# Ten early pairs per layer, later sums for the modulations, and a norm in seventeen steps

## The chip, the cores and the metric

The kernel runs on one core of a Trainium2 chip. The metric is the device time of one launch in microseconds (us). Five engines run their own streams of instructions: TensorE (PE in the profile; its weight loads are PEld), VectorE (DVE), ScalarE (ACT), GpSimd (POOL), and SyncE (SP), which here issues nearly all DMA transfers. They wait for each other through semaphores only.

## The reference

Two decoder layers over x (1024 tokens, 1024 features, float32). Layer 0 mixes tokens by sparse attention, layer 1 by a gated short convolution; both then have a SwiGLU feed-forward block. Each block's input is normed and modulated:

```python
mod = c_act @ ada_w[i] + ada_b[i]
sh1, sc1, g1, sh2, sc2, g2 = [m[:, None, :] for m in jnp.split(mod, 6, axis=-1)]
h = _rmsnorm(x, norm1_g[i]) * (1.0 + sc1) + sh1
x = x + g1 * mixer(h)                        # attention, or short convolution
h = _rmsnorm(x, norm2_g[i]) * (1.0 + sc2) + sh2
x = x + g2 * _swiglu(h, ffn_w_gate[i], ffn_w_up[i], ffn_w_down[i])
```

with `_swiglu` = (silu(h @ w_gate) * (h @ w_up)) @ w_down, hidden width 2816, and `_short_conv_mixer` = (b * conv3(c * u)) @ w_out, where b, c, u = split(h @ w_in).

## The kernel before

**Layout.** Activations are kept feature-major: 128 features on partitions, tokens along the free dimension, in two halves of 512 tokens. The residual stream is `xr`, 8 feature blocks by two halves. A float32 product is made as three matmuls on rounded parts (`mm3`): an operand is split into a high part (a cast, on ACT or DVE) and a low part (source minus high part, always on DVE), and hi·hi, hi·lo and lo·hi are added up in PSUM. So every operand of a product costs DVE at least one instruction of 128x512 (`wlo`, `alo` or a low half of `h..`/`t..`). Split weights stand in a ring of four units.

**Pairs.** In `Tail`, the products with `w_gate`, `w_up` and the convolution's `w_in` are made by a Strassen scheme with seven products in place of eight. A `Pair` is two column blocks of 128 of a weight matrix; its seven products use the operands h11, h21 (halves of the features, first 512 tokens), h22 and the combinations t1 to t4 (which need the second 512 tokens too). Each product is four blocks by three matmuls, twelve matmuls of 128x512. A feed-forward stage has 22 pairs (gate and up alternate), the convolution has 12.

An ordinary pair runs `first`, `second`, `rest`, `fourth`, `third` and adds its products up in PSUM. An *early* pair is begun before h22 and t1 to t4 exist: `early` makes its two products with h11 and h21 and stores their sum (p1 and c11, in tiles `cv`); later `done` makes the other five and adds the parts up on DVE. `EARLY` pairs of each stage begin early; the first `KEPT` = 4 of them stay in `cv` tiles, the others are written to DRAM by `put` (`aw..`) and read back by `get`. Early products give PE work while DVE and ACT make h22 and t1 to t4 in `norm_second`.

**Side steps.** The modulations of later blocks, mod = c_act @ ada_w, are computed beside other work: `side_step` loads 128 rows of `ada_w` for one half of one modulation (`adaw`, 256 KB) and adds them, scaled by one number per partition, to `adacc` (one DVE instruction). After eight such steps `ada_turned` transposes the sum on PE (`ps_sm<-ident,adacc`) and reduces it on DVE (`turned`). `SIDE` says how many steps follow each use of a pair in either layer; the list is in `run`.

**Down projection.** `down_pairs` multiplies the hidden rows, which lie in DRAM as `hid` and the sums `t1` to `t4`, by w_down, with the same scheme of seven products, in five loops over p = 0..10: one product per p in the first loop, two in the second and third, one in the fourth and in the fifth. `row()` fetches the next row tiles ahead of their use, up to `AHEAD` of them; `add_to` adds finished PSUM banks to `xr`, eight or four DVE instructions at a time. `between` is a generator of other work which is advanced inside the last two loops: in layer 0 it is the first norm of layer 1 (`norm_first`: squares on ACT, their sum on DVE, a reciprocal root, then per feature block one scaling and one low part on DVE), in layer 1 the output's transposes.

**What sets the order.** `Plan` records all instructions with their dependencies, and `drain` issues them: on each engine the one recorded first among those it expects to be ready, by its own table of costs. The result is a fixed program order on each engine. An engine works in that order: an instruction whose input is late holds up all behind it on the same engine, and on SP a DMA which waits for a free buffer holds up the DMAs behind it. Rings of tiles (`tp.tile(..., bufs=n)`) give their buffers in the order of recording.

All compute instructions are recorded by one helper, so nearly all have the line L244; groups are told apart by the names of their tiles.

## Time and profile before

| | us |
|---|---|
| median of three runs | 2328.48 |
| lowest and highest run | 2327.46, 2334.68 |
| the profiled execution | 2327.82 |
| span of its trace | 2325.6 |
| busy: PE, DVE, ACT | 2254.7, 1812.7, 1121.4 |

The stages behind the attention lie about here in the trace: first feed-forward stage from 673 to 1110, its down projection to 1345, the convolution from 1345 to 1580 and its output projection to 1680, the second feed-forward stage to 2100 and its down projection to the end. Matmuls are pipelined, so one shows some 390 ns of duration while the next begins 227 ns later; a stretch in which PE is busy without a break may still run at half clock, so the granted clock is read beside it (1.00 is full).

### The profile page before, as it was taken

What the parts mean: (1) busy time and instruction counts of PE and PEld (TensorE: products, weight loads), DVE (VectorE), ACT (ScalarE), POOL (GpSimd) and SP (SyncE); (2) the same over time, 40 slices, a digit from 0 to 9 for tenths busy, and PEclk for the clock granted to TensorE, in tenths of its full rate; (3) what the DMA queues carried; (4) which work ended last, traced back from release to release, by engine and by line L of the source; (5) the groups of instructions that cost most, each with busy time, mean ns of one, the idle gap of its engine ahead of it and who ended that gap; (6) DMA issues with size and microseconds to landing.
All of it is one profiled execution on the core that took longest, in us unless ns stands there. A gap on an engine that the chain in (4) does not pass through costs nothing.

```text
span 2325.6 us, 32943 instructions
## 1 busy us (share of the span) xinstructions
PE 2254.7 (97%) x11686; PEld 1821.2 (78%) x11686; DVE 1812.7 (78%) x3696; ACT 1121.4 (48%) x2140; POOL 5.6 (0%) x19
## 2 busy tenths in 40 slices
PE   7999999999999989999999899999999999999999
PEld 6657876776797768888888777788878888888887
DVE  6879999777488987777788689976799766667774
ACT  3576999757754333333344452233453333343444
POOL 0000000000000000000000000000000000000000
PEclk8999999999999999999999999999999999999999
DMA  8423333321243665555984134325346323349743
GB/s 294 128 64 94 98 110 101 117 82 57 83 137 110 201 194 168 169 181 190 368 322 169 55 109 127 91 87 176 91 118 199 127 95 114 104 140 390 274 137 95
DMA packets 324494, 346.92 MB, mean 149 GB/s; under 512 B 17609, under 2 KB 212202, under 8 KB 324330
## 3 DMA queue, kind: packets, MB, share of 16 engines
q1 hardware_dynamic: 322890, 343.52, 45.5%
q8 instruction: 91, 1.49, 0.3%
q10 hardware_dynamic: 1440, 1.31, 0.2%
q14 instruction: 73, 0.60, 0.1%
HBM read 276.35 MB, written 68.42 MB: 148 GB/s over the span
## 4 chain that ended last, share of the span: by engine, by line
PE 70%; DVE 14%; issue 7%; DMA 7%; ACT 2%; POOL 0%; SPq 0%; DVEq 0%; POOLq 0%; ACTq 0%
PE ps_x L244 28%; PE ps_mm L244 19%; PE ps_z L244 14%; PE ps_sm L244 5%; DVE u L244 2%; PE ps_L L244 2%; PE ps_o L244 2%; DVE s L244 2%; DVE v L244 2%; DVE wlo L244 2%; DVE p L244 1%; DMA raw<-in_conv_w_in_dram 1%; DMA raw<-in_ffn_w_gate_dram 1%; DVE sc L244 1%; DVE adacc L244 1%
## 5 line engine op out<-in xcount | busy, mean ns | idle before, releaser
L244 ACT CAST whi<-s 128x512 fp32r<-128x512 f32 x312 | 192.3, 621 | 471.1 <-DVE s L244 163.6
L244 PE MATMUL ps_x<-t,whi 128*128 128x512 f32 x1088 | 338.9, 392 | 5.1 <-ACT t L244 3.0
L244 ACT CAST whi<-raw 128x512 fp32r<-128x512 f32 (+1 forms) x245 | 149.9, 618 | 295.2 <-PE ps_z L244 89.5
L244 DVE TENSOR_TENSOR wlo<-s,whi 128x512 fp32r<-128x512 f32 x312 | 212.4, 684 | 43.3 <-ACT whi L244 42.7
L244 PEld LDWEIGHTS ps_x<-t,whi 128*128 128x128 f32 x1088 | 204.2, 188 | 49.2 <-ACT t L244 3.5
L244 DVE TENSOR_TENSOR wlo<-raw,whi 128x512 fp32r<-128x512 f32 (+1 forms) x254 | 173.0, 684 | 87.5 <-ACT whi L244 85.5
L244 PE MATMUL ps_x<-t,wlo 128*128 128x512 f32 x544 | 213.5, 393 | 4.8 <-DVE wlo L244 4.8
L244 PE MATMUL ps_x<-h,whi 128*128 128x512 f32 x512 | 158.7, 391 | 0.0
L244 PE MATMUL ps_z<-t,whi 128*128 128x512 f32 x472 | 146.6, 392 | 0.0
L244 PE MATMUL ps_z<-h,whi 128*128 128x512 f32 x424 | 130.6, 389 | 0.0
L244 DVE CUSTOM_DVE_ANT_0 p<-ps_L,bias 128x512 f32<-128x512 f32 (+3 forms) x192 | 99.8, 551 | 38.9 <-PE ps_L L244 24.0
L244 PE MATMUL ps_mm<-h,whi 128*128 128x512 f32 x408 | 126.2, 390 | 0.0
L244 DVE SCALAR_TENSOR_TENSOR adacc<-adaw,cact,adacc 128x512 f32<-128x512 f32 x140 | 104.5, 747 | 26.4 <-DMA adaw<-in_ada_w_dram 25.7
L244 PEld LDWEIGHTS ps_x<-t,wlo 128*128 128x128 f32 x544 | 102.7, 189 | 28.0 <-DVE wlo L244 6.5
L244 ACT ACTIVATE p<-p,nm,qsc 128x128 f32<-128x128 f32 (+7 forms) x128 | 112.2, 879 | 24.2 <-DVE nm L244 21.5
L244 PE MATMUL ps_x<-ph,whi 128*128 128x512 f32 x396 | 122.1, 389 | 0.0
L244 ACT ACTIVATE junk<-sc,bs 128x896 bf16<-128x896 f32 (+3 forms) x124 | 109.8, 885 | 14.2 <-DVE bs L244 9.6
L244 PEld LDWEIGHTS ps_x<-h,whi 128*128 128x128 f32 x512 | 96.5, 189 | 20.0
L244 DVE TENSOR_TENSOR s<-raw 128x512 f32<-128x512 f32 x112 | 76.0, 686 | 37.3 <-DMA raw<-in_ffn_w_gate_dram 20.6
L244 PEld LDWEIGHTS ps_z<-t,whi 128*128 128x128 f32 x472 | 89.2, 189 | 18.4
L244 PE MATMUL ps_x<-h,wlo 128*128 128x512 f32 x256 | 100.1, 391 | 0.0
L244 DVE TENSOR_TENSOR u<-u 128x512 f32<-128x512 f32 x143 | 97.1, 684 | 2.5 <-ACT u L244 0.8
(378 smaller groups left out, 5368.8 us busy)
## 6 DMA issues: line engine op xcount, KB each, us to landing
adaw<-in_ada_w_dram SPq DMA_DIRECT2D x160, 256.0 KB
ph<-in_ffn_w_down_dram SPq DMA_DIRECT2D x66, 512.0 KB
raw<-in_ffn_w_gate_dram SPq DMA_DIRECT2D x52, 512.0 KB
raw<-in_ffn_w_up_dram SPq DMA_DIRECT2D x52, 512.0 KB
rt<-t SPq DMA_DIRECT2D x80, 256.0 KB
raw<-in_conv_w_in_dram SPq DMA_DIRECT2D x32, 512.0 KB
hid<-u SPq DMA_DIRECT2D x52, 256.0 KB
rt<-hid SPq DMA_DIRECT2D x48, 256.0 KB
```

The costliest lines, as they stand in the source:

```text
L244: f(*[a.get() if isinstance(a, Ref) else a for a in args], **{k: a.get() if isinstance(a, Ref) else a for k, a in kw.items()})
```

## The change

1. `EARLY` is 10 in place of 8, in all three stages that use pairs; `KEPT` stays 4, so six pairs in place of four go to DRAM and come back.
2. The side steps begin at use n = 8 in place of n = 2. `SIDE` is (8, 4) in place of (5, 1). The list ends with modulation (1, 4) for layer 0's feed-forward stage; the last, (1, 5), is made in layer 1's. The sum lives in a `cv` tile of the ring of eight in place of a tile of its own, and `adaw` has three buffers in place of two. The turning of a finished sum is an entry of its own in the list, put after the third step of the next sum.
3. `norm_stat` becomes a generator, `norm_parts`. With `spread` (the down projection of layer 0) it gives way after each of its eight squares and begins with feature block 4, so the norm has 8 + 1 + 8 = 17 steps. In `down_pairs` the steps fall to p = 1 to 8 of the fourth loop and to the fifth loop, each behind that p's product.
4. In the third and fourth loop the first product is recorded before `add_to(other, ...)`, and in the third before the sums of the second product.
5. `AHEAD` is 8 in place of 24.

```diff
-    EARLY, KEPT, SIDE = 8, 4, (5, 1)
+    EARLY, KEPT, SIDE = 10, 4, (8, 4)
...
-    ROWS, AHEAD = ("t2", "t1", "t3", "t4", "h22"), 24
+    ROWS, AHEAD = ("t2", "t1", "t3", "t4", "h22"), 8
...
     def norm_stat(self, half, tag="sm", first=0):
+        *_, bc = self.norm_parts(half, tag, first)
+        return bc
+
+    def norm_parts(self, half, tag, first):
...
             acc = sq
+            yield
...
-        return self.tk.norm_bc(ss[:, 0:4], self.up, tag)
+        yield self.tk.norm_bc(ss[:, 0:4], self.up, tag)
...
-    def norm_first(self, layer, n, tag="sm"):
+    def norm_first(self, layer, n, tag="sm", spread=False):
 
-        bc = self.norm_stat(0, tag)
+        for bc in self.norm_parts(0, tag, 4 * spread):
+            if spread:
+                yield
...
+    def side_list(self, mods):
+
+        sets, steps = [(*m, half) for m in mods for half in range(NH)], []
+        for n, v in enumerate(sets):
+            for k in range(KT):
+                steps.append((v, k))
+                if n and k == 2:
+                    steps.append((sets[n - 1], KT))
+        return steps + [(sets[-1], KT)]
+
     def side_step(self):
         if not self.side:
             return
-        layer, j, half, k = self.side.pop(0)
+        (layer, j, half), k = self.side.pop(0)
         nc, tk = self.nc, self.tk
+        if k == KT:
+            tk.ada_turned(layer, j, self.acc.pop(0), half,
+                          self.sp.tile([P, 4], F32, name="turned", tag="turned", bufs=1))
+            return
         if k == 0:
-            self.acc = self.tp.tile([P, HW], F32, name="adacc", tag="adacc")
-        w = self.tp.tile([P, HW], F32, name="adaw", tag="adaw", bufs=2)
+            self.acc.append(self.cv())
+        w = self.tp.tile([P, HW], F32, name="adaw", tag="adaw", bufs=3)
...
         add_to(chain, (0, 1))
-        add_to(other, (1, 1))
         for p in range(n):
             (a11, a12), (a21, a22) = (load(2 * p, i, 2) for i in range(2))
             s3 = total(a11, a21, sub)
+            product(chain, p, s3, row(), True)
+            if p == 0:
+                add_to(other, (1, 1))
             s4 = total(s3, a22, sub)
             total(s4, a12, add, s4)
-            product(chain, p, s3, row(), True)
             product(other, p, s4, row(), True)
         add_to(chain, (1, 1))
-        add_to(other, (0, 1))
         for p in range(n):
-            if p < KT:
+            product(chain, p, late(2 * p + 1, 1), row(), True, tk.unit)
+            if p == 0:
+                add_to(other, (0, 1))
+            elif p <= KT:
                 next(between)
-            product(chain, p, late(2 * p + 1, 1), row(), True, tk.unit)
         add_to(chain, (1, 0))
         other = banks("mm", "mm", "x", "x")
         for p in range(n):
+            product(other, p, late(2 * p + 1, 0), row(), False, tk.unit)
             next(between, None)
-            product(other, p, late(2 * p + 1, 0), row(), False, tk.unit)
+        for _ in between:
+            pass
         add_to(other, (0, 0))
...
-            if f:
+            if n >= 8:
                 self.side_steps(layer)
...
-        self.side = [(layer, j, i, k) for layer, j in ((0, 5), *((1, j) for j in range(6)))
-                     for i in range(NH) for k in range(KT)]
+        self.side = self.side_list([(0, 5), *((1, j) for j in range(5))])
         self.ffn(0, w_gate[0], w_up[0])
-        self.down_pairs(w_down[0], 0, 5, self.norm_first(1, 0))
+        self.down_pairs(w_down[0], 0, 5, self.norm_first(1, 0, spread=True))
...
+        self.side = self.side_list([(1, 5)])
         self.ffn(1, w_gate[1], w_up[1])
```

The number of matmuls is the same in both kernels.

**How the order moves, at three places.** First SP, at the start of layer 0's feed-forward stage: `raw` are loads of weights (512 KB), `aw..<-cv` are the `put`s of early pairs, `cv<-aw..` the first `get`. Before:

```order
L244 DMA raw<-in_ffn_w_gate_dram 128x8x128
L244 DMA aw_0_190<-cv 128x512
L244 DMA aw_1_191<-cv 128x512
L244 DMA raw<-in_ffn_w_up_dram 128x8x128
L244 DMA raw<-in_ffn_w_gate_dram 128x8x128 x2
L244 DMA raw<-in_ffn_w_up_dram 128x8x128 x2
L244 DMA adaw<-in_ada_w_dram 128x512 x2
L244 DMA cv<-aw_0_184 128x512
```

In the changed kernel:

```order
L244 DMA aw_1_191<-cv 128x512
L244 DMA raw<-in_ffn_w_up_dram 128x8x128
L244 DMA aw_0_192<-cv 128x512
L244 DMA aw_1_193<-cv 128x512
L244 DMA raw<-in_ffn_w_gate_dram 128x8x128
L244 DMA aw_0_194<-cv 128x512
L244 DMA aw_1_195<-cv 128x512
L244 DMA raw<-in_ffn_w_up_dram 128x8x128
L244 DMA raw<-in_ffn_w_gate_dram 128x8x128 x2
L244 DMA raw<-in_ffn_w_up_dram 128x8x128 x2
L244 DMA cv<-aw_0_184 128x512
```

Two more pairs are put away, with two more loads, and no `adaw` stands between the weights of the first early pairs.

Second SP again, among layer 0's ordinary pairs: `raw` are the two halves of a pair's weights, `hid_..` and `t_..` rows that are stored. Before:

```order
L244 DMA adaw<-in_ada_w_dram 128x512 x2
L244 DMA raw<-in_ffn_w_gate_dram 128x8x128
L244 DMA adaw<-in_ada_w_dram 128x512 x2
L244 DMA raw<-in_ffn_w_gate_dram 128x8x128
L244 DMA hid_13_131<-u 128x512
L244 DMA raw<-in_ffn_w_up_dram 128x8x128
L244 DMA hid_13_109<-u 128x512
L244 DMA hid_12_130<-v 128x512
```

In the changed kernel:

```order
L244 DMA adaw<-in_ada_w_dram 128x512
L244 DMA raw<-in_ffn_w_gate_dram 128x8x128
L244 DMA adaw<-in_ada_w_dram 128x512 x8
L244 DMA raw<-in_ffn_w_gate_dram 128x8x128
L244 DMA adaw<-in_ada_w_dram 128x512 x3
L244 DMA hid_13_131<-u 128x512
L244 DMA raw<-in_ffn_w_up_dram 128x8x128
L244 DMA adaw<-in_ada_w_dram 128x512
L244 DMA hid_13_109<-u 128x512
L244 DMA adaw<-in_ada_w_dram 128x512 x4
L244 DMA hid_12_130<-v 128x512
```

Eight loads of `adaw` now stand between the two halves of one pair's weights where there were two.

Third DVE, in the last two loops of layer 0's down projection: `wlo` are low parts of a product's operands, `u<-xr,aff,ps_sm` the norm's scalings, `h_..` low parts of the normed rows (two tiles of four). Before:

```order
L244 TENSOR_TENSOR wlo<-rt_12017,whi 128x512
L244 SCALAR_TENSOR_TENSOR u<-xr,aff,ps_sm 128x512 x3
L244 SCALAR_TENSOR_TENSOR h_12692<-u,mod,h_12692 128x512
L244 SCALAR_TENSOR_TENSOR u<-xr,aff,ps_sm 128x512
L244 SCALAR_TENSOR_TENSOR h_12692<-u,mod,h_12692 128x512 x2
L244 SCALAR_TENSOR_TENSOR u<-xr,aff,ps_sm 128x512
L244 SCALAR_TENSOR_TENSOR h_12692<-u,mod,h_12692 128x512
L244 SCALAR_TENSOR_TENSOR u<-xr,aff,ps_sm 128x512
L244 SCALAR_TENSOR_TENSOR h_12556<-u,mod,h_12556 128x512
L244 SCALAR_TENSOR_TENSOR u<-xr,aff,ps_sm 128x512
L244 SCALAR_TENSOR_TENSOR h_12556<-u,mod,h_12556 128x512
L244 TENSOR_TENSOR wlo<-cv,whi 128x512
```

In the changed kernel, one loop later:

```order
L244 TENSOR_TENSOR wlo<-rt_12248,whi 128x512
L244 SCALAR_TENSOR_TENSOR u<-xr,aff,ps_sm 128x512 x3
L244 SCALAR_TENSOR_TENSOR h_12709<-u,mod,h_12709 128x512 x2
L244 TENSOR_TENSOR wlo<-cv,whi 128x512
L244 TENSOR_TENSOR wlo<-rt_12248,whi 128x512
L244 SCALAR_TENSOR_TENSOR h_12709<-u,mod,h_12709 128x512
L244 TENSOR_TENSOR wlo<-cv,whi 128x512
L244 TENSOR_TENSOR wlo<-rt_12248,whi 128x512
L244 SCALAR_TENSOR_TENSOR u<-xr,aff,ps_sm 128x512 x3
L244 TENSOR_TENSOR wlo<-cv,whi 128x512
```

Twelve norm instructions without a product's low part between them before, five at most now.

More of the change, by code (lines that the diff above doesn't have):

```diff
@@ L1396, in __init__ @@
                      for i in range(self.EARLY - self.KEPT)]
-        self.banks, self.side, self.b = 0, [], {}
+        self.banks, self.side, self.acc, self.b = 0, [], [], {}
     def bank(self):
@@ L1486, in side_step @@
             return
-        layer, j, half, k = self.side.pop(0)
+        (layer, j, half), k = self.side.pop(0)
         nc, tk = self.nc, self.tk
+        if k == KT:
+            tk.ada_turned(layer, j, self.acc.pop(0), half,
+                          self.sp.tile([P, 4], F32, name="turned", tag="turned", bufs=1))
+            return
         if k == 0:
-            self.acc = self.tp.tile([P, HW], F32, name="adacc", tag="adacc")
-        w = self.tp.tile([P, HW], F32, name="adaw", tag="adaw", bufs=2)
+            self.acc.append(self.cv())
+        w = self.tp.tile([P, HW], F32, name="adaw", tag="adaw", bufs=3)
         nc.sync.dma_start(w, tk.ada_rows(self.ada_w, layer, j, k)[:, half_of(half)])
-        tk.ada_step(w, k, self.acc)
-        if k == KT - 1:
-            tk.ada_turned(layer, j, self.acc, half,
-                          self.sp.tile([P, 4], F32, name="turned", tag="turned", bufs=1))
+        tk.ada_step(w, k, self.acc[-1])
     def side_steps(self, layer):
```

## The prediction

> **What bounds the kernel now.** I read the page's head first, then the stretches by stage, then who TensorE (PE) waited for, and last the rows of each wait. From the page:
>
> ```profile
> span 2325.6 us, 32943 instructions
> PE 2254.7 (97%) x11686; PEld 1821.2 (78%) x11686; DVE 1812.7 (78%) x3696; ACT 1121.4 (48%) x2140; POOL 5.6 (0%) x19
> ```
>
> PE is busy for 97% of the span, and the change leaves its matmuls as they are. So a gain can only come out of PE's idle time and out of stretches in which its clock is halved. The program starts to differ where the first feed-forward stage begins (about 673 us), so only the tail behind that counts. By stage (us of the window, then each engine's busy us, granted clock, DMA share, GB/s):
>
> ```profile
> 673.00:728.00 55.00, 51.71 (x232) 42.67 (x231) 52.64 (x91) 33.21 (x58) 0.00 (x0) 0.97 0.42 126
> 728.00:864.00 136.00, 126.96 (x542) 101.69 (x541) 119.62 (x200) 40.12 (x68) 0.00 (x0) 0.97 0.61 192
> 864.00:1100.00 236.00, 235.08 (x1052) 194.20 (x1051) 183.14 (x300) 82.62 (x144) 0.00 (x0) 1.00 0.54 175
> 1100.00:1210.00 110.00, 109.82 (x486) 90.33 (x484) 83.48 (x138) 45.16 (x80) 0.00 (x0) 1.00 1.00 360
> 1210.00:1270.00 60.00, 58.53 (x258) 48.16 (x257) 50.50 (x82) 22.90 (x41) 0.00 (x0) 1.00 0.51 180
> 1270.00:1320.00 50.00, 43.79 (x189) 35.57 (x188) 41.48 (x70) 27.83 (x48) 0.00 (x0) 0.93 0.18 64
> 1345.00:1403.00 58.00, 52.47 (x227) 41.98 (x226) 54.63 (x98) 32.90 (x59) 0.00 (x0) 0.94 0.38 109
> 1403.00:1510.00 107.00, 105.86 (x464) 86.24 (x463) 98.37 (x172) 26.56 (x46) 0.00 (x0) 1.00 0.40 118
> 1680.00:1732.00 52.00, 49.17 (x217) 40.02 (x217) 49.42 (x86) 31.87 (x56) 0.00 (x0) 0.97 0.36 108
> 1732.00:1840.00 108.00, 108.00 (x478) 89.39 (x478) 97.23 (x161) 36.70 (x63) 0.00 (x0) 1.00 0.55 171
> 1840.00:2090.00 250.00, 250.00 (x1106) 207.00 (x1105) 158.41 (x250) 90.71 (x155) 0.00 (x0) 1.00 0.35 113
> ```
>
> The first number is PE. It loses time at five places: the start of layer 0's feed-forward stage (673), its early pairs (728), the norm inside the first down projection (1270), the start of the convolution (1345) and the start of layer 1's feed-forward stage (1680). Who ended PE's waits from 660 to 2320, and the longest of them in place:
>
> ```profile
> PE ps_x L244 <- DVE wlo L244: 10.2, 4, 5.4
> PE ps_mm L244 <- DVE wlo L244: 8.1, 5, 3.9
> PE ps_sm L244 <- DVE adacc L244: 1.9, 1, 1.9
> 722.90 0.60 PE L244 MATMUL ps_x<-t,wlo 128*128 128x512 f32 x1 [3.29 <-DVE wlo L244]
> 819.37 0.79 PE L244 MATMUL ps_mm<-t,wlo 128*128 128x512 f32 x1 [3.87 <-DVE wlo L244]
> 1298.08 0.80 PE L244 MATMUL ps_x<-wlo,whi 128*128 128x512 f32 x1 [5.38 <-DVE wlo L244]
> 1394.59 0.50 PE L244 MATMUL ps_x<-t,whi 128*128 128x512 f32 x1 [3.04 <-ACT t L244]
> 1725.61 0.50 PE L244 MATMUL ps_mm<-t,wlo 128*128 128x512 f32 x1 [2.83 <-DVE wlo L244]
> ```
>
> PE waits for VectorE (DVE): a low part (`wlo`) of an operand comes late because DVE works on something else just then. The clock halves behind such waits; narrow stretches around four of them show idle time and clock together:
>
> ```profile
> 719.00:727.00 8.00, 4.71 (x14) 3.46 (x13) 8.00 (x15) 3.26 (x6) 0.00 (x0) 0.79 0.00 0
> 815.00:836.00 21.00, 14.26 (x50) 10.41 (x49) 17.60 (x30) 4.34 (x7) 0.00 (x0) 0.84 0.73 226
> 1292.00:1304.00 12.00, 6.62 (x19) 4.95 (x18) 9.85 (x16) 4.91 (x8) 0.00 (x0) 0.72 0.14 45
> 1391.00:1403.00 12.00, 6.47 (x17) 3.89 (x16) 12.00 (x23) 5.45 (x9) 0.00 (x0) 0.72 0.00 0
> 1722.00:1731.00 9.00, 6.17 (x22) 4.21 (x20) 9.00 (x16) 3.60 (x7) 0.00 (x0) 0.81 0.00 0
> ```
>
> Loss at a place = idle time + (1 − clock) × stretch. Start of layer 0: 3.29 + 0.21 × 8 = 5.0. Its early pairs: 136 − 126.96 = 9.0, and 0.16 × 21 = 3.4, so 12.4. Norm in the down projection: 50 − 43.79 = 6.2, and 0.28 × 12 = 3.4, so 9.6. Start of the convolution: 5.5 + 3.4 = 8.9. Start of layer 1: 2.83 + 0.19 × 9 = 4.5. The down projection's 1210 to 1270: 1.5. Together 41.9; some 2 go off where the halved clock falls on idle time, so **40 us** is all that can be won in these places.
>
> **The change part by part.**
>
> *Two more early pairs, in three stages.* A product is 12 matmuls:
>
> ```profile
> 860.21 8.16 PE ps_x L244 x36
> ```
>
> 36 in 8.16 is 0.227 us each, 2.72 a product. Two pairs bring four products, 10.9 us, to the place where DVE makes h22 and t1 to t4, and take them from a later one. They cost DVE there four low parts and two sums, six times 0.68 = 4.1 (rows below). DVE gains 10.9 − 4.1 = 6.8 us, against 3.3, 5.5 and 2.8 of idle time in 719, 1391 and 1722. So I take 0 left of 5.0 and of 4.5, and 1 left of 8.9 (bounds 0 and 7: there two sums more, of a norm that now ends later, come just before). Each such pair also ends with about four DVE adds more than an ordinary pair (done against third and rest), 2.7 us in stages that run DVE at 98.37 of 107 us: 0.3, for the two more of the convolution.
>
> New transfers: two puts and gets of two 256 KB tiles per pair and one more load of 512 KB, in three stages 24 × 0.25 + 6 × 0.5 = 9 MB. The stretches that take them use 0.42 to 0.61 of the DMA engines; I take 0. Uncovered, at the 192 GB/s of 728 to 864, they would be 47 us, which no row comes near.
>
> *Sums of modulations.* Of the side steps these rows show price and wait (864 to 1060, the same stage), and DVE's other kinds:
>
> ```profile
> L244 DVE SCALAR_TENSOR_TENSOR adacc<-adaw,cact,adacc 128x512 f32<-128x512 f32 x46 | 34.4, 747 | 7.3 <-DMA adaw<-in_ada_w_dram 6.9
> L244 DVE TENSOR_REDUCE turned<-ps_sm 128x4 f32<-128x512 f32 x7 | 4.8, 684 | 0.0
> L244 DVE SCALAR_TENSOR_TENSOR adacc<-adaw,cact,adacc 128x512 f32<-128x512 f32 x26 | 19.3, 744 | 0.3 <-DMA adaw<-in_ada_w_dram 0.3
> L244 DVE TENSOR_TENSOR wlo<-s,whi 128x512 fp32r<-128x512 f32 x34 | 22.9, 682 | 1.4 <-ACT whi L244 1.4
> SPq L244 <- DVE adacc L244: 39.7, 51, 2.4
> ```
>
> The third and fourth rows are of the early pairs, 728 to 864: 19.3 us of DVE go there to side steps, that is 2.4 a pair. All of it leaves the first eight pairs. Then DVE has 119.62 − 19.3 = 100 us for 127 of PE. Layer 1's same stretch, with one step per use, is the model: 97.23 of DVE in 108, and PE idle for nothing. I take 0 left of 12.4 there. Also, the turning transposes no longer stand right behind the last sum (the 1.9 on `adacc` above).
>
> What comes instead: uses 8 and 9 are early pairs (13.6 us of PE, 100 / 127 × 13.6 = 10.7 of DVE) and now carry eight entries each, 7.1 sums and 0.9 reductions: 7.1 × 0.747 + 0.9 × 0.684 = 5.9. DVE needs 16.6, 3.0 too much, 6 for two. Nobody waits for the sums soon, but DVE works in the written order. Bounds 0 and 6; I take 2.5. Then twelve ordinary pairs of 19.04: in layer 1 they need 158.41 / 250 × 19.04 = 12.1 of DVE, with 5.9 it is 18.0, plus the waits for `adaw` at DVE's head. These are now 6.9 us for 46 steps, 0.15 each: 7.1 × 0.15 = 1.1. That makes 19.1: DVE and PE even. Bounds: 0, and with a doubled wait 12 × (18.0 + 2.1 − 19.04) = 13. I take 5, between the row's 0.15 and its double, since three buffers hold their rows now, but SP issues up to eight of these loads in one run ahead of a weight load. For halved clock here 1.7 more, as behind the 2.83 wait.
>
> On that 1.7 a rule of the Trainium skill differs. "TensorE: Matmul & The Clock Gate", Part 1 (the HAM clock gate), says the clock halves after an idle window of about 3.4 us. Here waits of 2.83 and 3.29 us were followed by 0.81 and 0.79, so the trace is harsher; by the page the 1.7 falls away and the forecast would be 2298.
>
> *The norm in seventeen steps.* Now (at 1287 to 1296) the scaled rows come in one run:
>
> ```profile
> L244 DVE SCALAR_TENSOR_TENSOR h<-u,mod,h 128x512 fp32r<-128x512 f32 x8 | 5.9, 745 | 0.0
> L244 DVE SCALAR_TENSOR_TENSOR u<-xr,aff,ps_sm 128x512 f32<-128x512 f32 x8 | 5.8, 742 | 0.3 <-PE ps_sm L244 0.3
> 1320.00:1345.00 25.00, 25.00 (x112) 20.71 (x111) 13.00 (x21) 11.38 (x21) 0.00 (x0) 1.00 0.03 11
> ```
>
> 11.7 us, of which twelve instructions stand together (about 8.9) with no low part between them; PE can be at most two products, 5.4 us, ahead. In the new order at most five stand together, 3.7 us, less than 5.4. They move to the last pass, where DVE now has 12 of 25 us free. That pass then needs 22 × 0.68 + 16 × 0.745 + 4 × 0.743 = 29.9 of 11 × 2.72 = 29.9 us: full, though runs of instructions overlap by some 0.08 each. I take 0.5 left of 9.6; bounds 0 and 3.
>
> *Order within the down projection; rows fetched eight ahead in place of 24.* A product now goes ahead of the sums and of the adds: of 1.5 us I leave 0.5. Eight rows are 8 × 2.72 = 22 us of lead; I take 0, and at most 2.
>
> Sum of what stays: 1 + 0.3 + 2.5 + 5 + 1.7 + 0.5 + 0.5 = 11.5. Gain 40 − 11.5 = 28.5. The profiled execution took 2327.82 us, 2.2 outside its span, and is 0.66 below the median of 2328.48. So 2328.5 − 28.5 = **2300 us**.
>
> **Rivals.**
>
> *DVE becomes the bound of layer 0's ordinary pairs (other side).* Place: uses 10 to 21. SP issues in order and waits for DVE to free an `adaw` buffer (39.7 us in 51 waits today); eight in a run hold up the second half of the next pair's weights, whose sums DVE then waits for, and PE behind it. Loss = 12 × (18.0 + 7.1 w − 19.04), with w the wait per step, in place of the 5 above: 0.15 gives 0, 0.30 gives 13 (2308), 0.47 gives 28 (2323); from about 0.55 the kernel is slower than before, and at 0.7 the loss is 47, 2295 + 47 = 2342. For it: DVE at 95% with no spare. Against it: the third buffer, and a stage that moves 175 GB/s where the next one moves 360. In the Trainium skill's "DMA: Bandwidth & Descriptors", Latency and other measured facts, HBM access is 0.2 us on average and 2 us under high load; that would speak for a growing w, and no row here parts it from queueing.
>
> *The early pairs stay short.* If the waits at 728 to 864 come from the weights' two buffers and not from the side steps, 12.4 stay: 2312. Against it: layer 1's stretch, whole with the same two buffers.
>
> *The norm only moves.* If the full last pass runs late by 3 us and the convolution's first product behind it, 5 to 8 of the 18 come back: 2306.
>
> *The starts don't heal.* If the extra products find their own low parts late, 5.0, 8.9 and 4.5 stay: 2317. Against it: 6.8 us of room against at most 5.5.
>
> **How the numbers follow.** Forecast (2288 to 2307) 0.55; norm only moves 0.10; early pairs stay short 0.10; starts don't heal 0.05; DVE bound 0.20, of which half ends within 7 us of before and half slower. What can be told from no change here is 0.3%, 7 us. So faster 0.80, same 0.10, slower 0.10. Range: all 40 won gives 2288; upwards the rivals of 2306, 2312 and 2317 and the lighter part of the DVE rival come in: **2288 to 2322**.
>
> **What would show it.** Right: PE busy for whole stretches around the three starts and around the first down projection's norm, clock 1.00 there; DVE near 95% in layer 0's ordinary pairs with PE still whole. Wrong: PE waits on `wlo` between 840 and 1090 with DVE waiting for `adaw` or for weights (the first rival); waits among layer 0's first eight uses (the second); a gap where the convolution's first product starts (the third). A new wait of the rows of the down projection on DMA would show that eight ahead is too few.

## The result, and the profile after

The changed kernel takes **2303.85 us** (median of four runs, 2300.25 to 2306.35) against 2327.97 for the kernel before (four runs: the three of the table ahead and one more): a ratio of 0.9894, 95% interval 0.988 to 0.9908. That is 24.1 us less, where 28.5 were forecast. The profiled execution took 2300.25 us. From its page:

```profile
span 2298.5 us, 33032 instructions
PE 2239.1 (97%) x11686; PEld 1812.2 (79%) x11686; DVE 1822.3 (79%) x3716; ACT 1116.4 (49%) x2137; POOL 5.6 (0%) x19
```

By stage (window in us, its length, then busy us of PE, PEld, DVE, ACT, POOL with counts, granted clock, DMA share, GB/s):

```profile
673.00:728.00 55.00, 55.00 (x252) 45.79 (x251) 51.12 (x89) 34.03 (x59) 0.00 (x0) 1.00 0.49 144
728.00:837.00 109.00, 109.00 (x482) 90.25 (x482) 93.40 (x154) 37.31 (x64) 0.00 (x0) 1.00 0.56 175
837.00:1093.00 256.00, 245.65 (x1094) 200.52 (x1093) 219.91 (x362) 84.90 (x150) 0.00 (x0) 1.00 0.62 201
864.00:1093.00 229.00, 220.25 (x983) 179.77 (x982) 193.52 (x319) 76.88 (x136) 0.00 (x0) 1.00 0.61 199
1260.00:1310.00 50.00, 49.97 (x230) 41.56 (x229) 40.55 (x70) 28.03 (x49) 0.00 (x0) 1.00 0.20 69
1335.00:1393.00 58.00, 56.71 (x250) 46.33 (x249) 56.92 (x96) 32.66 (x58) 0.00 (x0) 1.00 0.47 136
1393.00:1510.00 117.00, 114.59 (x498) 92.50 (x497) 107.73 (x190) 28.30 (x47) 0.00 (x0) 1.00 0.39 115
1655.00:1707.00 52.00, 52.00 (x235) 43.17 (x234) 49.72 (x85) 32.48 (x56) 0.00 (x0) 1.00 0.49 141
1843.00:2070.00 227.00, 224.64 (x994) 185.33 (x993) 145.86 (x232) 81.51 (x141) 0.00 (x0) 1.00 0.38 123
```

PE is whole at the three places that were to heal without a remainder (673, 1260, 1655), nearly whole at the convolution's start (1335), and the clock is 1.00 in all of them. The new loss is in layer 0's uses 8 to 21, that is the last two early pairs and the ordinary ones, among which the side steps now lie: 256 − 245.65 = 10.35 us of idle time from 837 to 1093, in eight waits. Who ended most of them:

```profile
PE ps_x L244 <- ACT v L244: 6.3, 4, 2.7
PE ps_mm L244 <- DVE u L244: 1.6, 1, 1.6
```

Behind the other 2.4 us are DVE's sums `u` (1.8) and one `wlo` (0.6). So it is mostly no longer a `wlo` that is late, but what empties a PSUM bank. The longest wait, with the end of an earlier product and some of what DVE, ACT and SP did just before it (start in us, duration, engine, instruction, count, in brackets the idle time before it and what ended it):

```profile
974.62 0.38 SPq L244 DMA_DIRECT2D raw<-in_ffn_w_gate_dram  x1
974.98 0.39 PE L244 MATMUL ps_z<-h,wlo 128*128 128x512 f32 x1
975.58 8.76 SPq L244 DMA_DIRECT2D adaw<-in_ada_w_dram  x7
979.69 1.54 DVE L244 SCALAR_TENSOR_TENSOR cv<-adaw,cact,cv 128x512 f32<-128x512 f32 x2 [0.29 <-DMA adaw<-in_ada_w_dram]
981.15 0.68 DVE L244 TENSOR_TENSOR v<-v,ps_z 128x512 f32<-128x512 f32 x1
981.86 0.63 ACT L244 ACTIVATE v<-v 128x512 f32<-128x512 f32 x1 [2.72 <-DVE v L244]
982.91 0.57 ACT L244 COPY v<-ps_x 128x512 f32<-128x512 f32 x1
983.54 0.73 PE L244 MATMUL ps_x<-t,whi 128*128 128x512 f32 x2 [2.73 <-ACT v L244]
984.62 0.38 SPq L244 DMA_DIRECT2D raw<-in_ffn_w_gate_dram  x1
```

Read it from the bottom. PE needs the bank `ps_x`, which ACT copies out at 982.91. ACT's copy stands behind its activation of `v`, which waited 2.72 us for DVE's sum of `v` (981.15). That sum adds up `ps_z`, whose last matmul of the pair before (974.98) was over at 975.4: it comes 5.8 us late. In these 5.8 us DVE idles for 0.4 and spends 3.1 on side sums that stand ahead of it, the rest on sums and low parts of weights. So the place of the side sums in DVE's order shows here, more than a wait for `adaw` at that moment. In the first five ordinary pairs this sum is 4.3 to 7.1 us late. SP meanwhile spends 8.76 us on seven `adaw` loads between the two halves of one pair's weights. These loads and weights keep DVE waiting too, which puts it behind with everything that follows. What DVE waited for in the same 837 to 1093:

```profile
DVE s L244 <- DMA raw<-in_ffn_w_gate_dram: 12.5, 5, 3.7
DVE cv L244 <- DMA adaw<-in_ada_w_dram: 10.5, 16, 1.7
DVE s L244 <- DMA raw<-in_ffn_w_up_dram: 5.5, 5, 2.0
```

To compare kernels whose stages begin at different times, the table below takes the same piece of work in each profiled execution: the time from the start of a stage's first 128x512 matmul to that of its 241st (20 products of twelve), from there to the 841st (70 products), and so on, worked out from the trace's start times. At full pace (0.227 us a matmul) 20 products are 54.5 us, 50 are 136, 84 are 229. A piece also holds small matmuls: a start has 16 of the norm and takes 56.3 with PE never idle; a turned sum has four transposes, some 0.13 us each. Pieces of kernels that differ nowhere near them vary by up to 3 us: layer 0's "84 others" by 1.8 (244.9, and 246.7 in e4_ahead24), "the others" of the convolution from 179.4 (e9_pool) to 182.3 (e4_ahead24).

| us | before | after | early8 | norm9 | side2 | resident | side2_adaw2 | side2_early8 |
|---|---|---|---|---|---|---|---|---|
| layer 0's pairs: first 20 products | 61.7 | 56.3 | 62.7 | 56.3 | 56.3 | 56.3 | 56.3 | 62.6 |
| to the 70th | 152.5 | 138.2 | 139.5 | 136.8 | 145.6 | 136.4 | 156.4 | 149.7 |
| the 84 others | 233.6 | 244.9 | 242.1 | 246.6 | 238.4 | 235.9 | 244.3 | 232.6 |
| its down projection | 223.1 | 211.5 | 211.5 | 220.5 | 211.5 | 211.5 | 211.5 | 211.5 |
| convolution's pairs: first 20 | 65.0 | 56.2 | 65.2 | 56.3 | 56.2 | 56.8 | 56.2 | 64.8 |
| the others | 176.5 | 181.7 | 178.8 | 179.6 | 180.3 | 179.5 | 181.4 | 180.9 |
| layer 1's pairs: first 20 | 61.6 | 56.3 | 62.6 | 56.3 | 56.3 | 56.3 | 56.3 | 61.3 |
| to the 70th | 136.0 | 136.0 | 143.9 | 137.6 | 137.0 | 136.0 | 137.0 | 138.1 |
| the 84 others | 229.0 | 232.4 | 229.5 | 232.8 | 228.5 | 232.6 | 228.5 | 228.5 |

The columns behind "after" are experiments (their labels without the number), told next.

### The profile page after: what moved, and what is told of

It reads as the page before. It is cut to its first block, busy times and chain, and to the rows that moved or that the text cites. A ratio compares the mean times of both kernels' runs of the same rounds, so it can differ in the third digit from the quotient of the medians.

```text
span 2298.5 us, 33032 instructions
## 1 busy us (share of the span) xinstructions
PE 2239.1 (97%) x11686; PEld 1812.2 (79%) x11686; DVE 1822.3 (79%) x3716; ACT 1116.4 (49%) x2137; POOL 5.6 (0%) x19
## 3 DMA queue, kind: packets, MB, share of 16 engines
q10 hardware_dynamic: 1440, 1.31, 0.2%
## 4 chain that ended last, share of the span: by engine, by line
PE 62%; DVE 18%; DMA 9%; issue 8%; ACT 2%; SPq 0%; POOL 0%; DVEq 0%; ACTq 0%; POOLq 0%
PE ps_x L244 24%; PE ps_mm L244 17%; PE ps_z L244 12%; PE ps_sm L244 5%; DVE s L244 3%; DVE u L244 3%; DVE wlo L244 3%; DMA raw<-in_ffn_w_gate_dram 2%; PE ps_L L244 2%; PE ps_o L244 2%; DVE v L244 2%; DMA adaw<-in_ada_w_dram 2%; DMA raw<-in_conv_w_in_dram 2%; DMA raw<-in_ffn_w_up_dram 2%; DVE cv L244 2%
## 5 line engine op out<-in xcount | busy, mean ns | idle before, releaser
L244 PE MATMUL ps_x<-t,whi 128*128 128x512 f32 x1016 | 315.2, 391 | 8.6 <-ACT v L244 7.3
L244 PEld LDWEIGHTS ps_x<-t,whi 128*128 128x128 f32 x1016 | 189.2, 188 | 50.6 <-ACT v L244 9.4
L244 PE MATMUL ps_x<-t,wlo 128*128 128x512 f32 x508 | 198.2, 390 | 0.2 <-DVE wlo L244 0.2
L244 PE MATMUL ps_x<-h,whi 128*128 128x512 f32 x536 | 165.6, 390 | 0.0
L244 PE MATMUL ps_z<-h,whi 128*128 128x512 f32 x408 | 125.8, 389 | 1.1 <-DVE u L244 1.1
L244 PEld LDWEIGHTS ps_x<-t,wlo 128*128 128x128 f32 x508 | 95.3, 188 | 21.2 <-DVE wlo L244 1.0
L244 DVE TENSOR_TENSOR u<-u 128x512 f32<-128x512 f32 x152 | 102.9, 684 | 2.4 <-ACT u L244 0.8
L244 PE MATMUL ps_mm<-hhi,whi 128*128 128x512 f32 (+2 forms) x240 | 93.5, 391 | 1.6 <-ACT hhi L244 1.6
```

The source lines that it names most:

```text
L244: f(*[a.get() if isinstance(a, Ref) else a for a in args], **{k: a.get() if isinstance(a, Ref) else a for k, a in kw.items()})
```

## The experiments

Every ratio is against the kernel before on the same chip, with its 95% interval; the diffs are against the changed kernel. The changed kernel itself was not run again beside them, so it is compared with them through the two ratios.

| run | edit | median us | before us | ratio |
|---|---|---|---|---|
| e1_early8 | eight early pairs | 2323.97 | 2333.13 | 0.9961 (0.9948–0.9974) |
| e2_norm9 | norm in nine steps, ahead of the products | 2315.61 | 2333.13 | 0.992 (0.9899–0.9942) |
| e3_side2 | side steps from use 2, six per use | 2303.0 | 2333.13 | 0.987 (0.9854–0.9886) |
| e4_ahead24 | rows fetched 24 ahead | 2308.44 | 2333.13 | 0.9892 (0.9876–0.9907) |
| e5_resident | side sums without their loads | 2294.57 | 2333.12 | 0.9841 (0.9826–0.9855) |
| e6_one_of_eight | 7 of 8 side steps left out | 2292.87 | 2333.12 | 0.9835 (0.982–0.9849) |
| e7_side2_turn | e3, turned at once | 2301.28 | 2333.12 | 0.9868 (0.9851–0.9884) |
| e8_side0 | side steps from use 0, five per use | 2306.52 | 2333.12 | 0.9896 (0.988–0.9913) |
| e9_pool | `adaw` loads issued by GpSimd | 2304.05 | 2329.72 | 0.9882 (0.9863–0.9901) |
| e10_pool_side2 | e3, loads issued by GpSimd | 2309.57 | 2329.72 | 0.9911 (0.9895–0.9927) |
| e11_side2_adaw2 | e3, two `adaw` buffers | 2319.76 | 2329.72 | 0.9958 (0.9942–0.9974) |
| e12_side2_early8 | e3, eight early pairs | 2320.46 | 2329.72 | 0.9963 (0.9951–0.9976) |

**The parts one by one.** The first four runs each undo one part: is the gain the early pairs', the norm's, the side steps' or the rows'?

*Eight early pairs.*

```diff
-    EARLY, KEPT, SIDE = 10, 4, (8, 4)
+    EARLY, KEPT, SIDE = 8, 4, (8, 4)
```

> The changed kernel with 8 early pairs per stage in place of 10; all else as changed (side steps from use 8, norm in 17 steps, rows 8 ahead). Theory (the two more pairs cover the making of h22 and t1 to t4): the waits at the three starts come back with their halved clocks, 5.0 + 8.9 + 4.5 = 18 us, so 2304 + 18 = 2322 us, with PE idle 3 us or more at the first five-product pair of each of the three stages. Rival (the starts were late because side sums and the burst of the norm stood in DVE's way, and those are gone anyway): 2304 to 2309 us, no wait over 2 us at a start.

The ratio is 0.0067 above that of the changed kernel, 15.6 us; by the table the profiled execution lost 22.3. The three starts lose again what they lost before. PE's first matmul behind each wait, and one more wait that layer 1 shows here (1834):

```profile
725.22 0.79 PE L244 MATMUL ps_x<-t,wlo 128*128 128x512 f32 x1 [3.27 <-DVE wlo L244]
1381.79 0.50 PE L244 MATMUL ps_x<-t,whi 128*128 128x512 f32 x1 [3.06 <-ACT t L244]
1715.11 0.80 PE L244 MATMUL ps_mm<-t,wlo 128*128 128x512 f32 x1 [3.27 <-DVE wlo L244]
1834.43 0.80 PE L244 MATMUL ps_z<-t,wlo 128*128 128x512 f32 x1 [4.12 <-DVE wlo L244]
```

First-20 rows of the table: 62.7, 65.2 and 62.6 against 56.3, 56.2 and 56.3, together 21.7. Those are the two more early pairs, and nothing else in the change heals these starts. Meanwhile "to the 70th" stays at 139.5, so with the late side steps layer 0's early pairs do not need the ten.

*The norm in nine steps.* The old order of the fourth loop, sums included, and of the fifth, with `spread` off:

```diff
+        add_to(other, (0, 1))
         for p in range(n):
-            product(chain, p, late(2 * p + 1, 1), row(), True, tk.unit)
-            if p == 0:
-                add_to(other, (0, 1))
-            elif p <= KT:
+            if p < KT:
                 next(between)
+            product(chain, p, late(2 * p + 1, 1), row(), True, tk.unit)
...
-        self.down_pairs(w_down[0], 0, 5, self.norm_first(1, 0, spread=True))
+        self.down_pairs(w_down[0], 0, 5, self.norm_first(1, 0))
```

> The changed kernel with the first norm of layer 1 in 9 steps again (its sum of squares in one piece, all in the fourth loop of the down projection) and the steps ahead of the product as before; all else as changed. Theory (twelve norm instructions in a row on DVE are longer than the two products that PE has in store): PE waits some 5 us in the fourth loop and its clock halves, 6.2 + 3.4 = 9.6 us, so 2313 us. Rival (the norm only moves: the full fifth loop gives the time back at the convolution's start): 2304 us, within 3, with the wait in the fourth loop there but the convolution's start better by as much.

The old wait is back to the hundredth, and so is the halved clock. First PE's matmul behind it, then a narrow window with the clock:

```profile
1294.86 0.80 PE L244 MATMUL ps_x<-wlo,whi 128*128 128x512 f32 x1 [5.38 <-DVE wlo L244]
```

```profile
1290.00:1302.00 12.00, 7.14 (x22) 5.74 (x23) 8.63 (x14) 4.09 (x7) 0.00 (x0) 0.72 0.20 66
```

The down projection takes 220.5 in place of 211.5: 9.0. The convolution is 2.0 shorter (56.3 + 179.6 against 56.2 + 181.7), but 179.6 lies within the 179.4 to 182.3 of kernels that keep the seventeen steps. So it is not shown that anything of what the longer norm saves comes back one stage later. By the ratios the part is worth 0.0026, 6 us; those intervals overlap, so its size rests on the profile.

*Side steps from use 2, rows 24 ahead.*

```diff
-    EARLY, KEPT, SIDE = 10, 4, (8, 4)
+    EARLY, KEPT, SIDE = 10, 4, (6, 4)
...
-            if n >= 8:
+            if n >= 2:
                 self.side_steps(layer)
```

> The changed kernel with the side steps from use 2 on as before the change, six per use (20 uses for 108 entries) in place of eight from use 8; all else as changed. Theory (two opposite terms): the early pairs of layer 0 lose up to 12.4 us again, the ordinary pairs get their 10 us of waits back (PE idle between 837 and 1093 now), so about 2306 us (2300 to 2312): late side steps as such are worth little. Rival A (the side steps among the early pairs were the loss, the ordinary pairs' waits have another cause): 2316 us. Rival B (the early pairs' waits were the weights' two buffers and healed through other parts): 2294 us.

```diff
-    ROWS, AHEAD = ("t2", "t1", "t3", "t4", "h22"), 8
+    ROWS, AHEAD = ("t2", "t1", "t3", "t4", "h22"), 24
```

> The changed kernel with rows of the down projection fetched 24 ahead as before; all else as changed. Theory (eight ahead cost and bring nothing, PE is whole in the down projection either way): 2304 us, within 3. Rival (fewer transfers in a burst at 1100 to 1210 is part of the gain): 2309 us or more, with PE waiting for weights or rows between 1090 and 1260.

The rows make no difference (0.9892 against 0.9894). The late beginning does not help as a whole: with side steps from use 2 the ratio is 0.987, lower by 0.0024 (5.6 us, the intervals just overlap). Two windows of e3_side2, the first eight uses and the ordinary pairs:

```profile
728.00:837.00 109.00, 106.81 (x473) 87.15 (x473) 104.13 (x175) 35.77 (x60) 0.00 (x0) 1.00 0.67 214
864.00:1093.00 229.00, 225.35 (x995) 184.48 (x995) 182.04 (x300) 77.07 (x135) 0.00 (x0) 0.99 0.55 177
```

The first uses lose 2.2 us in this window where the changed kernel loses none, and the ordinary pairs 3.65 where it loses 8.75. The table takes the early pairs whole, beyond the window's end: "to the 70th" is 145.6 against 138.2, 7.4 us of price (some 2 of them the transposes of four more turned sums). The 84 others are 6.5 shorter for it. Over the whole of layer 0's pairs the two are even (440.3 against 439.4). What e3 gains lies in layer 1's ordinary pairs (228.5 against 232.4), from which the sixteen steps of the last modulation are gone; its early pairs, which now have them, take 1.0 more. So **in layer 0 moving the side steps moves their price and does not lower it**. A later beginning does heal the early pairs, then, but what it heals there is paid behind them. What is the price?

**What the side steps cost.** One run keeps the sums and drops their loads; the other drops seven of eight steps.

```diff
+        self.fixed = None
...
-        w = self.tp.tile([P, HW], F32, name="adaw", tag="adaw", bufs=3)
-        nc.sync.dma_start(w, tk.ada_rows(self.ada_w, layer, j, k)[:, half_of(half)])
-        tk.ada_step(w, k, self.acc[-1])
+        if self.fixed is None:
+            self.fixed = self.tp.tile([P, HW], F32, name="adaw", tag="adaw", bufs=1)
+            nc.sync.dma_start(self.fixed, tk.ada_rows(self.ada_w, layer, j, k)[:, half_of(half)])
+        tk.ada_step(self.fixed, k, self.acc[-1])
```

> The changed kernel with every side step reading one resident tile (loaded once) in place of its own rows of the modulation weights: DVE's sums, their number and place stay, 111 of 112 loads go. (The modulations are then sums of the wrong rows.) Cause in question: the 10 us in which PE waits between 837 and 1093 of the changed kernel. Theory D (DVE is simply full with 8 entries per use): the waits stay, ratio to before 0.988 to 0.990 (2304 where before is 2328). Theory S (SP's runs of loads and the waits of DVE for them hold up weights and sums): 7 of the 10 us go, ratio 0.986 (2296 to 2298).

```diff
-        if k == 0:
-            self.acc.append(self.cv())
+        if k:
+            return
+        self.acc.append(self.cv())
```

> The changed kernel with seven of eight side steps left out, loads and sums (the modulations are then an eighth of their sums). Both theories: the whole price of the side steps falls away, PE has no wait over 1 us between 700 and 1090, ratio 0.985 (2293 where before is 2328). If waits of 5 us or more stay there, neither loads nor sums are their cause, but the ordinary pairs' own start behind ten early ones.

Seven eighths of the steps gone bring 0.0059, 13.7 us. The loads alone bring 0.0053, 12.3. DVE's sums all run in e5_resident, and DVE is even busier there, yet in layer 0 PE waits for next to nothing:

```profile
837.00:1093.00 256.00, 254.68 (x1141) 210.17 (x1140) 230.13 (x379) 88.75 (x155) 0.00 (x0) 1.00 0.35 112
```

DVE is busy for 230.13 of 256 us (90%) with PE idle for 1.3; in the changed kernel it was 219.91 (86%) with 10.35. A DVE that is too full is thus not what PE waits for in layer 0; it is what the loads bring with them. The run doesn't part the wait for a load from the place which the planner gives a sum because of its load, since it changes both: the sum of `v` in the chain above comes at most 2.7 us late here, with at most 1.5 us of side sums ahead of it.

In layer 1 it is otherwise. Its 84 others take 232.6 with resident rows and 232.4 with loads, and PE waits as long without the loads (2.6 us against 2.4). From 1700 to 2085 in e5_resident:

```profile
PE ps_mm L244 <- DVE v L244: 1.6, 1, 1.6
PE ps_x L244 <- ACT v L244: 1.0, 1, 1.0
```

With seven of eight steps left out PE doesn't wait there and the piece takes 229.5. So in layer 1 the price is that of the sums, or of their place, and not of the loads.

**Which side of the loads.** They can hurt in three ways: on SP, where they stand ahead of weights; in DVE, which waits for them in its order; or through too few buffers. First SP: let GpSimd issue them.

```diff
-        nc.sync.dma_start(w, tk.ada_rows(self.ada_w, layer, j, k)[:, half_of(half)])
+        nc.gpsimd.dma_start(w, tk.ada_rows(self.ada_w, layer, j, k)[:, half_of(half)])
```

> The changed kernel with the side steps' loads issued by GpSimd in place of SP; their number, buffers, sums and places stay. The run with a resident tile showed that the loads make the 10 us of waits among layer 0's ordinary pairs. Theory Q (order on SP: a load that waits for a free buffer holds up the weights behind it): the waits fall below 3 us, ratio to before 0.985 to 0.987. Theory B (the bytes themselves, or DVE's waits for them: the DMA engines carry as much as before): the waits stay, ratio 0.989 to 0.990.

No clear difference (0.9882 against 0.9894). PE's idle time from 837 to 1093 is 8.2 in place of 10.35, where theory Q had under 3, and DVE has traded one wait for another:

```profile
837.00:1093.00 256.00, 247.83 (x1099) 203.08 (x1098) 223.67 (x369) 82.71 (x145) 49.33 (x92) 0.99 0.63 202
```

```profile
DVE cv L244 <- DMA adaw<-in_ada_w_dram: 16.3, 16, 3.1
DVE s L244 <- DMA raw<-in_ffn_w_gate_dram: 8.4, 4, 4.4
DVE s L244 <- DMA raw<-in_ffn_w_up_dram: 4.3, 4, 2.4
```

The waits for weights fell from 18.0 to 12.7 us, those for `adaw` rose from 10.5 to 16.3. So the order on SP is not the whole of it. The Trainium skill, "DMA: Bandwidth & Descriptors", Specifications, puts the latency to the first byte at about 1 us for a transfer issued on GpSimd's path and about 0.6 on SP's. DVE's waits for `adaw` grew in this direction, sixteen in both kernels, 0.66 us each in the changed kernel and 1.02 here; but such a wait is not the latency itself, and no run here shows that latency for SP's loads.

The same with the steps from use 2, and two ways of placing them otherwise:

> Side steps from use 2, six per use, with their loads issued by GpSimd: a try at a kernel faster than both. By theory Q the 5 us among the early pairs and the 4 of one wait and its halved clock among the ordinary ones go down by half: ratio 0.984 to 0.985, against 0.987 with SP. By theory B 0.987 as with SP.

```diff
             for k in range(KT):
                 steps.append((v, k))
-                if n and k == 2:
-                    steps.append((sets[n - 1], KT))
-        return steps + [(sets[-1], KT)]
+            steps.append((v, KT))
+        return steps
```

> The kernel with side steps from use 2, six per use (ratio 0.987 to before), with the turning of each sum put right behind its eighth step again, as before the change; all else the same. It asks why the early pairs of layer 0 lost 12.4 us with such steps before the change and lose 5 now with more of them. Theory (PE stands in order behind a transpose whose sum is late; before, one such wait was 1.9 us and the DVE work behind it late): 3 to 6 us come back, ratio 0.989. Rival (the third buffer or the two more early pairs healed it): 0.987 as without this edit.

```diff
-    EARLY, KEPT, SIDE = 10, 4, (8, 4)
+    EARLY, KEPT, SIDE = 10, 4, (5, 4)
...
-            if n >= 8:
+            if n >= 0:
                 self.side_steps(layer)
```

> The changed kernel with side steps from the first use, five per use (22 uses for 108 entries): the thinnest spread. Theory (what costs is the number per use, 5.9 us of DVE in 19 at eight entries against 3.7 at five): waits among ordinary pairs go to under 1 us, those among the ten early pairs stay near 5 us, ratio 0.986 to 0.987 (2297). Rival (side steps among the first early pairs meet DVE's full load from the three starts): the early pairs lose over 8 us, ratio 0.989 or more.

Loads by GpSimd make e3 slower, 0.9911 against 0.987: a miss as an improvement, and against the theory that SP's order is the price. Turning a sum at once costs nothing (0.9868 against 0.987). From use 0 the ratio is 0.9896: worse than from use 2. Layer 0's early pairs then lose time in many small waits ("to the 70th" 153.7), but get most of it back behind them (232.0; together 442.0 against 440.3). More is lost in layer 1, where the edit also moves the steps to the first uses: "to the 70th" is 140.9 there against 137.0.

**Buffers.** e3 with two `adaw` buffers, as the kernel before had; and with eight early pairs.

```diff
-        w = self.tp.tile([P, HW], F32, name="adaw", tag="adaw", bufs=3)
+        w = self.tp.tile([P, HW], F32, name="adaw", tag="adaw", bufs=2)
```

> Side steps from use 2, six per use (ratio 0.987), with two buffers for their rows as before the change in place of three. It asks what healed the early pairs of layer 0, which lost 12.4 us before the change with fewer side steps than here. Theory (the third buffer: SP stands less often behind a full pair of buffers): layer 0's first feed-forward stage gets 4 to 8 us longer, ratio 0.989 to 0.990. Rival (not the buffers): 0.987.

Two buffers cost 0.0088, 20 us, more than any theory had. Of that 16.7 are in layer 0's pairs (457.0 against 440.3). PE's matmuls behind the two longest waits:

```profile
824.41 0.80 PE L244 MATMUL ps_z<-t,wlo 128*128 128x512 f32 x1 [6.90 <-DVE wlo L244]
1046.23 1.22 PE L244 MATMUL ps_x<-t,whi 128*128 128x512 f32 x2 [4.92 <-ACT v L244]
```

And what DVE and SP waited for from 728 to 870, in e11_side2_adaw2:

```profile
DVE whi L244 <- DMA raw<-in_ffn_w_gate_dram: 5.9, 4, 2.0
DVE whi L244 <- DMA raw<-in_ffn_w_up_dram: 5.9, 3, 2.7
SPq L244 <- DMA adaw<-in_ada_w_dram: 22.3, 11, 4.4
```

in e3_side2, with three:

```profile
DVE whi L244 <- DMA raw<-in_ffn_w_up_dram: 2.0, 1, 2.0
DVE whi L244 <- DMA raw<-in_ffn_w_gate_dram: 1.2, 1, 1.2
SPq L244 <- DMA adaw<-in_ada_w_dram: 7.0, 6, 2.8
```

and in the kernel before, with two:

```profile
DVE whi L244 <- DMA raw<-in_ffn_w_gate_dram: 5.2, 2, 3.3
DVE whi L244 <- DMA raw<-in_ffn_w_up_dram: 4.3, 2, 2.3
SPq L244 <- DMA adaw<-in_ada_w_dram: 8.3, 5, 3.3
```

With two buffers SP waits for `adaw` itself, the next weights are issued late behind that, and DVE's `whi` and then its `wlo` come late. DVE's waits in the kernel before are like that (9.5 us, against 11.8 and 3.2 here). SP's are not: its 8.3 lie near the 7.0 of the run with three buffers. So it is not shown that this chain made the loss of the kernel before.

```diff
-    EARLY, KEPT, SIDE = 10, 4, (6, 4)
+    EARLY, KEPT, SIDE = 8, 4, (6, 4)
```

> Side steps from use 2, six per use, with 8 early pairs per stage. The other candidate for the healed early pairs of layer 0. Theory (the two more early pairs heal only the starts): ratio 0.987 + 0.0066 (the 15.5 us that 8 early pairs cost in the run with late side steps) = 0.9935, and the first feed-forward stage is 5 to 6 us longer than with ten. Rival (they also heal the early pairs' own waits): that stage is 12 us longer or more, as long as before the change, ratio 0.996.

Eight early pairs cost 0.0093 here, 21.7 us, more than in the first experiment. That is the rival's ratio, but not by the rival's way: in the table the three starts take 6.3 + 8.6 + 5.0 = 19.9 us more than in e3, while layer 0's pairs as a whole, start included, take only 4.6 more, close to the theory's 5 to 6. Layer 0's two windows (compare the same windows of the kernel before, 126.96 and 235.08):

```profile
728.00:864.00 136.00, 128.52 (x555) 101.60 (x554) 124.56 (x210) 41.20 (x70) 0.00 (x0) 1.00 0.66 208
864.00:1100.00 236.00, 236.00 (x1057) 195.07 (x1056) 187.01 (x306) 83.15 (x145) 0.00 (x0) 1.00 0.54 175
```

This kernel has as many early pairs as the one before, side steps from the same use, more of them per use, and a third buffer. It loses 7.5 us from 728 to 864 in short waits at full clock, where the kernel before lost 12.4. The long waits are gone from that stretch, as between e11 and e3 (6.90 us against 1.31). How much of the 12.4 it would have taken by itself in the kernel before stays open: e12 also has six steps per use and turns a sum later. Set beside e1, which differs from e12 in where the side steps begin and how many follow a use, it shows what the late beginning is worth with eight early pairs: "to the 70th" falls from 149.7 to 139.5, and the 84 others rise from 232.6 to 242.1.

The best kernels of this study are e7_side2_turn and e3_side2, 0.9868 and 0.987. Both are clearly faster than the kernel before; against the changed kernel they are some 5 to 6 us ahead, with intervals that just overlap.

## Why the prediction was right, and where it wasn't

The forecast of 2300 us, the range of 2288 to 2322 and the likeliest case (faster) held. The terms of its sum against the table, as gain of the changed kernel over the one before:

| place | predicted | measured |
|---|---|---|
| start of layer 0's pairs | 5.0 | 61.7 − 56.3 = 5.4 |
| the rest of layer 0's pairs | 12.4 − 2.5 − 5 − 1.7 = 3.2 | 14.3 − 11.3 = 3.0 |
| its down projection | 9.6 + 1.5 − 0.5 − 0.5 = 10.1 | 223.1 − 211.5 = 11.6 |
| the convolution | 8.9 − 1 − 0.3 = 7.6 | 8.8 − 5.2 = 3.6 |
| start of layer 1's pairs | 4.5 | 61.6 − 56.3 = 5.3 |
| behind it in layer 1 | 0 | 229.0 − 232.4 = −3.4 |

**Two more early pairs: right, mechanism and size.** The starts came out whole, and e1 loses these gains again. The nine megabytes of new transfers are not seen there: PE is whole from 673 to 728 and from 1655 to 1707.

**Norm in seventeen steps: right.** 11.6 us, of which e2 shows 9.0 to be the norm's with the order of its loops; the last pass stays whole. Nothing shows that the rival "the norm only moves" has a part in it.

**Early pairs of layer 0: the step right, its account incomplete.** "All of it leaves the first eight pairs … I take 0 left of 12.4" came out: PE is whole from 728 to 837. The late beginning, with eight steps a use in place of six, is worth 7.4 us there with ten early pairs (e3) and 10.2 with eight (e12 against e1). The sum left out two things. The price moves into the pairs behind, nearly whole (6.5 and 9.5 us). And a third buffer heals the same pairs while the steps stay among them: 156.4 to 145.6 (e11, e3). DVE's 19.3 us of side sums can't have been the whole reason either: in e12 DVE is busier than in the kernel before (124.56 against 119.62) and PE loses less. DVE's waits for weights in 728 to 864 of before, 9.5 us, are no term of the sum. I held the buffers of the weights to be a rival and not those of `adaw`.

That the row behind the start comes out (3.0 for 3.2) is luck in part. Worked out were a gain of 12.4 − 2.5 = 9.9 and a loss of 5 + 1.7 = 6.7; measured were 14.3 and 11.3. Of each some 1.6 are twelve transposes of turned sums that went from the one piece to the other.

**Ordinary pairs of layer 0: a loss at the named place, for another reason, and larger.** I took 5 for them, 2.5 for uses 8 and 9, and 1.7 for a halved clock. PE was idle for 10.35 us at a clock of 1.00, 1.60 of them in uses 8 and 9. The step that failed is "DVE and PE even": DVE was to need 18.0 of 19.04 us a pair beside its waits. It was busy for 193.52 of 229, that is 16.1 a pair, and PE waited all the same; in e5 DVE is fuller and PE hardly waits. "DVE near 95% with PE still whole", the sign of being right, did not appear. The wait per step came out as forecast for the light case; the group of 864 to 1060:

```profile
L244 DVE SCALAR_TENSOR_TENSOR cv<-adaw,cact,cv 128x512 f32<-128x512 f32 x69 | 51.6, 748 | 10.2 <-DMA adaw<-in_ada_w_dram 9.4
```

9.4 / 69 = 0.14. By the rival's formula that w gives 0, and still 10 us were lost. A sum over averages misses them: the loss is made of eight single delays of 0.65 to 2.73 us. Four, 6.3 us together, are a late DVE sum, an ACT waiting for it and a bank not emptied; the others wait for DVE directly. The rival's place was right, and the waits that it named (DVE's for `adaw` and for weights) are there. Its price was not right, and its chain is not shown to make the loss: with the loads off SP (e9) 8.2 us stay. What remains open is whether the waits for the loads or the places of the sums make it.

**The halved clock.** The 1.7 fell away: the longest wait, 2.73 us, left the clock at 1.00. That doesn't speak for the rule of the Trainium skill that the prediction cites: a wait of 2.50 us in the same stage of e3_side2 is followed by half clock (0.99 over its window). The last section has the rest. It could as well have cost what I took.

**The convolution: 4 us short.** One us was left at its start, where PE is never idle (the 1.8 above full pace are the norm's small matmuls). Behind the start 0.3 were taken for the two more done pairs' adds, and 5.2 were lost. The window 1393 to 1510 shows DVE busy for 107.73 of 117 us and PE idle for 2.4. The norm is not shown to be the cause: the piece takes 179.6 in e2 and 179.4 to 182.3 in the kernels with seventeen steps, against 176.5 before. Nor is the number of early pairs: with eight it is 178.8 in e1 and 180.9 in e12. The cause stays open.

**Layer 1's ordinary pairs: not foreseen.** Side steps also move there, to four a use from use 8 on, in place of one a use from use 2 on. I costed only layer 0's. In e3, with the same four a use from use 2 on, the 3.4 us are gone (228.5). They are not the loads' (e5, 232.6).

**Fewer rows ahead, later turning: nothing,** as predicted for the rows (e4). I had the later turning take away the wait of 1.9 on `adacc`; e7, which turns at once, is no slower.

The sum fell short by 4 us: the convolution (4.0) and layer 1 (3.4) too dear, the down projection and the two starts a little better than forecast. Of the 27.1 us between the two profiled spans 2.5 lie ahead of anything that the change touches: the first feed-forward stage begins at 671.1 in place of 673.6, and between 671 and 681 in the fourteen profiles.

## What to carry to other kernels

When an engine's work seems too much beside another's, take away its inputs' transfers before moving its work. In layer 0 that took PE's idle time from 10.35 us to 1.3 while all the sums stayed; in layer 1 the same trial showed that the loads were not the price. Moving work may only move its price, so look at the stage as a whole and not only at the place that was healed. A prefetch ring on a DMA queue that works in order must be deep enough that the queue seldom waits for it, since whatever stands behind (here the weights) inherits the wait; one more 256 KB buffer was worth 20 us where the loads lie among the early pairs. And a busy share of 86% with waits, beside 90% without, says that an average of work per pair can't tell whether an engine delivers on time; look at the single waits and at what stands ahead of the late instruction.

## What the runs showed of the hardware

**The clock halves behind shorter waits than I had seen.** I took all of PE's waits over 1.5 us in the tails of the fourteen profiles, and read from the distance of the matmuls behind each (0.43 us in place of 0.23) whether the clock was halved. Two of 1.84 and one of 1.96 fell into a clock that was halved already. Of the others, 14 between 1.53 and 1.89 left it full, 19 of 2.83 and longer were all followed by half clock, and between 1.92 and 2.73 it was six of eight. Two of that middle: a wait of 2.01 in e10_pool_side2 that halved it, and that of 2.73 in the changed kernel (shown above, at 983) that did not. First the one in e10 with its window:

```profile
808.84 0.73 PE L244 MATMUL ps_z<-t,whi 128*128 128x512 f32 x2 [2.01 <-ACT whi L244]
```

```profile
808.00:815.00 7.00, 5.83 (x17) 4.38 (x18) 7.00 (x13) 4.44 (x8) 0.82 (x2) 0.76 0.63 189
```

then the window of the changed kernel:

```profile
983.00:990.00 7.00, 6.46 (x28) 5.37 (x29) 3.18 (x6) 2.11 (x5) 0.00 (x0) 1.00 0.67 209
```

So these runs show no one threshold, but a stretch from 1.9 to 2.8 us in which it may go either way. The Trainium skill's "TensorE: Matmul & The Clock Gate", Part 1, has the clock halve after at least one idle window of about 3.4 us; the traces disagree, with halved clock behind waits down to 1.92. What decides between two waits of the same length is open.

**GpSimd as an issuer.** A load of 256 KB issued there took 3.5 us from issue to landing (median of 112), and it occupied GpSimd for 0.54 us (e9_pool; its page gives no time to landing for SP's loads, so the two can't be compared):

```profile
L244 POOL DMA_DIRECT2D adaw<-in_ada_w_dram x112 | 60.2, 538 | 1591.8 <-DVE cv L244 1144.2
adaw<-in_ada_w_dram POOLq DMA_DIRECT2D x112, 256.0 KB, 3.5
```
